# Keeping attention's tile pool open through the up phase, and storing W1's block sums of four groups for the second token half

## The chip, the cores and the metric

The kernel runs on one core of one Trainium2 chip. The metric is the device time of one execution in microseconds (us). A core has five engines that run their own instruction queues: TensorE (PE in the profile, with its weight loads as PEld), VectorE (DVE), ScalarE (ACT), GpSimd (POOL) and SyncE (SP), which here only issues DMA transfers. A transfer issued on SP keeps its place in SP's queue: where it has to wait, everything behind it waits too.

## The reference

One encoder layer over 2048 tokens of width 1024, all in fp32: two mixers in parallel (a Hyena convolution and a bidirectional mLSTM), an output projection, cross-attention into 256 memory tokens, and a feed-forward block of width 4096. Cut to what matters here:

```python
h = h + mixed @ w_out[l]
h = h + _cross_attention(_rms_norm(h, norm_x_g[l]), _rms_norm(mem, norm_mem_g[l]),
                         xa_wq[l], xa_wk[l], xa_wv[l], xa_wo[l])
h = h + jnp.square(jax.nn.relu(_rms_norm(h, norm_ff_g[l]) @ ff_w1[l])) @ ff_w2[l]
...
return _rms_norm(h, final_norm_g)
```

The change lies in the third line, in the product with `ff_w1` (the up phase), and at the end of the second line.

## The kernel before

Every fp32 operand of a product is split into a high part `h` (a cast to fp32r on ACT) and a low part `l` (the rest, a subtraction on DVE or POOL), and one product of blocks is three matmuls: high by high (L340), low by high (L341) and high by low (L342). Names ending in `h` and `l` are these parts: `ah`, `al` of a W1 block, `xh`, `xl` or `bh`, `bl` of a block of tokens.

**Up.** The product with W1 is done in blocks with seven products in place of eight (a Strassen scheme, as `ORDER_UP = (1, 2, 6, 7, 5, 4, 3)`). The tokens come in two halves (`tp` 0 and 1), W1 in 16 groups of columns. For each token half there are seven x operands, one for each product, some of them sums of blocks of x that attention has left in DRAM (`xs`), the others blocks of `hg`, attention's output times the norm's gain. They are split once and then used by all 16 groups. For each group and product there is one W1 operand: four blocks are loaded (L1578), and POOL makes four sums out of them in place (`s` at L1581, `t[1,0]` at L1582, `t[0,0]` at L1590, `t[0,1]` at L1592). One step is one product of one group, four 128x512 blocks deep, and so 12 matmuls; there are 224 steps. The order of the steps is written out as a list: in each token half the first two groups are taken together product by product, the others one by one, and at the end of the first half again two together (14 and 15). In the steps of group 15 of the first half the x operand that has just had its last use is replaced by that of the second half (`ffn_x`). W1 operands are split two steps ahead. The products of a group are added up by DVE (`plus` L1666, `fin` L1671, with two activations L1672 and L1673), POOL makes four sums of the results (L1721 to L1724), and all are stored to DRAM as `hc` (L1662), where the down phase loads them (`wr<-hc`).

**Tile pools.** `T` ("t") belongs to w_out and attention: weights as they come (`wn`, four tiles), their halves `wh` and `wl` (two each), activations `act` (four tiles of 16 KB a partition) and the accumulator `acc` (16 KB). It is closed at the end of attention, and the pool `U` ("up") opens in its place, with the x operands of products 2 to 7, the results `q`, the running sums `u` (six) and the POOL sums `t` (four). `R` ("ring") holds the raw loads `wr` (six slots) and the halves `ah`, `al` (four) and `bh`, `bl` (six). `C` ("wring") holds 12 tiles `w` for W1 blocks. A tile that is asked for waits until the last reader of its slot is done.

**From attention to up.** In attention's last column of tokens (`c == 3`), at its fifth block of output columns (`ct == 4`), `ffn_pre` loads and splits the operands of product 1: x into `bh`, `bl`, and the W1 blocks of products 1 and 2 of groups 0 and 1. It also loads x for product 2 without splitting it. The other x operands are split in the first 12 steps of up, when `U` is there. After the last output block, attention's store of the row statistics `mb` (made by DVE at L1517, stored by SP at L1518) ends that phase; `hg` is stored by ACT's queue (L1488) and the residual by SP (L1490).

The order on each engine is set by a scheduler at build time, from the order of the program, dependencies and its own estimate of each instruction; the pools' slots decide what can be asked for early. `mm3` is the three matmuls, `halves` (L1539, L1540) the split of one block, `raw` (L1534) a load into the ring.

Of the kernel before, what the change touches and what calls it, by code (L numbers as in the profile page):

```python
# [10 lines left out]
F32 = mybir.dt.float32  # L11
F32R = mybir.dt.float32r
# [121 lines left out]
class Prog:  # L134
# [1173 lines left out]
    def attention(self, es):  # L1308
        nc, tc, a = self.nc, self.tc, self.a
# [7 lines left out]
        T = self.T  # L1317
# [51 lines left out]
        mix = mixed(0)  # L1369
        y = next(mix)  # L1370
        stats = None
        acc = T.tile([128, 8, 512], F32, name="acc")
        for c in range(4):

            def residual(h):
# [116 lines left out]
            for ct in range(8):  # L1492
                yield 5.2
                if ct % 2 == 0:
                    w = next(wst) if ct else w
                else:
                    k = sums.pop(0) if sums else None
                    if k is not None:
                        self.sums_x(A, k, "sm")
                if c == 3 and ct == 4:  # L1500
                    self.ffn_pre()
                p = gemm(w, ct, o, half[ct], range(4, 8)) if ct < 2 else gemm(w, ct % 2, o)
                if prev is not None:
                    finish(ct - 1, prev, ssum)
                    store(ct - 1)
                prev = p
# [36 lines left out]
    def ffn_open(self, es):  # L1543
        es.enter_context(self.tc.tile_pool(name="even", bufs=1, side="right")).tile([128, 120], F32, name="even")
        self.R = es.enter_context(self.tc.tile_pool(name="ring", bufs=1, side="right"))
        self.xt = {}
        self.W, self.WD = {}, {}

    def ffn_xload(self, tp, i):
# [3 lines left out]
        return [self.raw(xs[tp, where, :, k] if isinstance(where, int) else hg[2 * tp + where[1], :, 4 * where[0] + k])  # L1553
                for k in range(4)]

    def ffn_x(self, pool, i, src):
        nc = self.nc
        eng = (nc.vector, nc.gpsimd)
        if i == 1:
            self.xt[i] = [self.halves(x, ("bh", "bl"), 6, eng[k % 2]) for k, x in enumerate(src)]  # L1560
            return
        hi, lo = (pool.tile([128, 4, 512], F32R, name=f"x{n}{i}", tag=f"x{n}{i}") for n in "hl")
        for k, raw in enumerate(src):
            nc.scalar.copy(hi[:, k], raw)
            eng[k % 2].tensor_tensor(lo[:, k], raw, hi[:, k].bitcast(F32), ALU.subtract)
        self.xt[i] = [(hi[:, k], lo[:, k]) for k in range(4)]

    def wtile(self):
        return self.C.tile([128, 512], F32, tag="w", name="w", bufs=12)

    def load_w1(self, g):
        op = self.nc.gpsimd.tensor_tensor
        b = self.blocks_of(1, g)
        t = self.W[g] = {}
        for m in (0, 1):
            for k in (1, 0):
                x = self.wtile()
                self.nc.sync.dma_start(out=x.rearrange("p (k c) -> p k c", k=4), in_=b[m][k])  # L1578
                t[m, k] = x
        t["s"] = self.wtile()  # L1580
        op(t["s"], t[1, 0], t[1, 1], ALU.add)  # L1581
        op(t[1, 0], t[0, 0], t[1, 0], ALU.subtract)  # L1582

    def ffn_w1(self, tp, g, i):
        op = self.nc.gpsimd.tensor_tensor
        if i == 1:
            self.load_w1(g)
        t = self.W[g]
        if i == 6:
            op(t[0, 0], t["s"], t[0, 0], ALU.subtract)  # L1590
        if i == 3:
            op(t[0, 1], t[0, 1], t[0, 0], ALU.subtract)  # L1592
        src = t[{1: (0, 0), 2: (0, 1), 6: (0, 0), 7: (1, 0), 5: "s", 4: (1, 1), 3: (0, 1)}[i]]
        return [x.rearrange("p (k c) -> p k c", k=4) for x in self.halves(src, ("ah", "al"), 4, self.nc.vector)]

    def ffn_pre(self):
        self.ffn_x(self.R, 1, self.ffn_xload(0, 1))
        self.wq = []
        for k in range(2):
            for g in range(2):  # L1600
                t = self.R.tile([128, 512], F32, tag="wr", name="wr", bufs=6)
                v = t.rearrange("p (k c) -> p k c", k=4)
                self.nc.sync.dma_start(out=v, in_=self.blocks_of(1, g)[0][k])
                w = self.halves(t, ("ah", "al"), 4, self.nc.vector)
                self.wq.append([x.rearrange("p (k c) -> p k c", k=4) for x in w])
        self.xraw = self.ffn_xload(0, 2)

    def ffn_product(self, aa, i):
        x = self.xt[i]
# [5 lines left out]
    def ffn(self):  # L1615
# [2 lines left out]
        groups = [(0, (0, 1))] + [(0, (g,)) for g in range(2, 14)] + [(0, (14, 15)), (1, (0, 1))]  # L1618
        groups += [(1, (g,)) for g in range(2, 16)]
        steps = [(tp, g, i) for tp, gs in groups for i in self.ORDER_UP for g in gs]  # L1620
        self.C = self.ctx.enter_context(tc.tile_pool(name="wring", bufs=1))
        prods = [(o, i) for o in range(4) for i in self.ORDER_DOWN]
        down = [(n, tp, k) for n in range(len(prods)) for tp in range(2) for k in range(4)]
        aq, bq = {}, {}
# [30 lines left out]
            bq[s] = self.halves(self.raw(hc[tp, i - 1, 4 * o + k]), ("bh", "bl"), 6, eng)  # L1655

        with tc.tile_pool(name="up", bufs=1) as U:
            def tmp():
                return U.tile([128, 512], F32, tag="u", name="u", bufs=6)

            def out(tp, g, j, t):
                nc.sync.dma_start(out=hc[tp, j - 1, g], in_=t)  # L1662

            def plus(p, other):
                t = tmp()
                nc.vector.tensor_tensor(t, p, other, ALU.add)  # L1666
                return t

            def fin(p, other, tp, g, j):
                c = U.tile([128, 512], F32, tag="q", name="q", bufs=7)  # L1670
                nc.vector.tensor_tensor(c, p, other, ALU.add)  # L1671
                nc.scalar.activation(c, c, AF.Relu)  # L1672
                nc.scalar.activation(c, c, AF.Square)  # L1673
                if j:
                    out(tp, g, j, c)
                return c

            wq = self.wq
            xsum = list(range(4, 8))
            us, cs = {}, {}  # L1680
            for n, (tp, g, i) in enumerate(steps):
                if n < 2:
                    self.load_w1(n)
                if n < 12 and n % 2 == 0:
                    j = self.ORDER_UP[n // 2 + 1]
                    self.ffn_x(U, j, self.ffn_xload(0, j) if n else self.xraw)
                if 4 <= n + 2 < len(steps):
                    wq.append(self.ffn_w1(*steps[n + 2]))
                if n + 9 >= len(steps) and n + 5 < len(steps):
                    load_w(0, n + 9 - len(steps))  # L1690
                if n + 2 >= len(steps):
                    k = n + 2 - len(steps)
                    fetch_b(k)
                    fetch_a(0, k)
                if i == 4 and xsum and g % 2 and 2 < g < 13:
                    self.sums_x(U, xsum.pop(0), "t")
                bank = self.ffn_product(wq.pop(0), i) if n > 1 else self.first[n]
                u, c = us.setdefault(g, {}), cs.setdefault(g, {})
                if i == 1:
                    u[1] = tmp()  # L1700
                    nc.scalar.copy(u[1], bank)
                elif i == 2:
                    c[11] = fin(bank, u[1], tp, g, 1)
                elif i == 6:
                    u[2] = plus(bank, u[1])
                elif i == 7:
                    u[3] = plus(bank, u[2])
                elif i == 5:
                    c[22] = fin(bank, u[3], tp, g, 3)
                    u[4] = plus(bank, u[2])  # L1710
                elif i == 4:
                    c[21] = fin(bank, u[3], tp, g, 2)
                else:
                    c[12] = fin(bank, u[4], tp, g, 0)
                    if n + 1 == len(steps):
                        fetch_a(0, 2)
                        fetch_b(2)
                        fetch_a(0, 3)
                    t = [U.tile([128, 512], F32, tag="t", name="t", bufs=4) for _ in range(4)]
                    op = nc.gpsimd.tensor_tensor  # L1720
                    op(t[0], c[12], c[11], ALU.subtract)  # L1721
                    op(t[1], c[22], t[0], ALU.subtract)
                    op(t[2], c[22], c[12], ALU.subtract)
                    op(t[3], c[21], t[1], ALU.subtract)  # L1724
                    for j, x in zip((5, 6, 7, 4), t):
                        out(tp, g, j, x)
                if g == 15 and tp == 0:
                    self.ffn_x(U, i, self.ffn_xload(1, i))
        h2 = self.dram("h2", (4, 128, 8, 512))
        msd = self.dram("msd", (4, 128, 512))  # L1730
        with tc.tile_pool(name="down", bufs=1) as B:
# [155 lines left out]
def program(p):  # L1887
    with ExitStack() as ms:
        with ExitStack() as es:
# [18 lines left out]
            for _ in take(m, 1):  # L1908
                pass
        with ExitStack() as rs:  # L1910
            with ExitStack() as at:
                p.tail_open(at)
                g = p.attention(at)
                weave(g, m, 440, 96, True)
                ms.close()
                p.ffn_open(rs)
                for _ in g:
                    pass
            p.ffn()
# [48 lines left out]
```

## Time and profile before

| | us |
|---|---|
| median of 3 runs | 3202.12 |
| lowest and highest run | 3199.16 and 3203.77 |
| the profiled execution's own time | 3198.5 |
| span of the profiled execution | 3196.7 |
| TensorE busy | 3040.7 |
| DVE busy | 2067.3 |
| ACT busy | 1502.0 |
| POOL busy | 1184.8 |

The span runs from the first to the last instruction that the profiler records; the execution's own time is 1.8 us longer. The mean granted clock of TensorE was 0.982 of full speed. In a line of the profile, `xl<-wr,xh` says what is written from what by the program's names, `x4` counts instructions that the view joins, and the brackets at the end say how long the engine stood idle before and what released it.

### The profile page before, as it was taken

What the parts mean: (1) busy time and instruction counts of PE and PEld (TensorE: products, weight loads), DVE (VectorE), ACT (ScalarE), POOL (GpSimd) and SP (SyncE); (2) the same over time, 40 slices, a digit from 0 to 9 for tenths busy, and PEclk for the clock granted to TensorE, in tenths of its full rate; (3) what the DMA queues carried; (4) which work ended last, traced back from release to release, by engine and by line L of the source; (5) the groups of instructions that cost most, each with busy time, mean ns of one, the idle gap of its engine ahead of it and who ended that gap; (6) DMA issues with size and microseconds to landing.
All of it is one profiled execution on the core that took longest, in us unless ns stands there. A gap on an engine that the chain in (4) does not pass through costs nothing.

```text
span 3196.7 us, 43569 instructions
## 1 busy us (share of the span) xinstructions
PE 3040.7 (95%) x14473; PEld 2391.2 (75%) x14473; DVE 2067.3 (65%) x3563; ACT 1502.0 (47%) x2873; POOL 1184.8 (37%) x818
## 2 busy tenths in 40 slices
PE   6999999999999976999999998999999999999998
PEld 5655566776667766888878887888788878888876
DVE  7775366344874767877775547666655676555695
ACT  5543366424774344454444445555555443333335
POOL 0122012100121334324151218777766483434483
PEclk9999999999999988999999999999999999999999
DMA  5554766686677987556384437655544474444434
GB/s 186 196 198 168 252 195 209 171 266 197 170 231 209 300 269 236 171 169 207 108 295 150 162 120 243 210 195 188 193 153 157 147 248 156 139 135 149 125 93 168
DMA packets 445177, 602.14 MB, mean 188 GB/s; under 512 B 38670, under 2 KB 250766, under 8 KB 443928
## 3 DMA queue, kind: packets, MB, share of 16 engines
q1 hardware_dynamic: 406772, 540.84, 53.2%
q10 hardware_dynamic: 38180, 58.51, 5.5%
q8 instruction: 115, 1.88, 0.2%
q14 instruction: 110, 0.90, 0.1%
HBM read 401.00 MB, written 198.21 MB: 187 GB/s over the span
## 4 chain that ended last, share of the span: by engine, by line
PE 77%; DMA 9%; DVE 7%; issue 3%; ACT 2%; POOL 1%; SPq 1%; ACTq 0%; DVEq 0%; POOLq 0%
PE mm L340 16%; PE mm L341 16%; PE mm L342 16%; PE hy L342 5%; PE hy L340 5%; PE hy L341 5%; PE hy L177 3%; PE hy L876 2%; PE mm L845 1%; PE hy L918 1%; DVE bl L1540 1%; DVE wl L345 1%; PE hy L1082 1%; PE hy L1213 1%; DMA wn<-in_xa_wq_t_dram 1%
## 5 line engine op out<-in xcount | busy, mean ns | idle before, releaser
L345 DVE TENSOR_TENSOR wl<-wn,wh 128x512 fp32r<-128x512 f32 (+1 forms) x364 | 285.7, 820 | 115.8 <-ACT wh L345 115.8
L1540 DVE TENSOR_TENSOR bl<-wr,bh 128x512 fp32r<-128x512 f32 x213 | 236.3, 1115 | 130.8 <-ACT bh L1539 127.1
L345 ACT CAST wh<-wn 128x512 fp32r<-128x512 f32 (+1 forms) x364 | 208.2, 619 | 232.2 <-PE mm L342 56.2
L1539 ACT CAST ah<-w 128x512 fp32r<-128x512 f32 x284 | 176.2, 622 | 300.0 <-PE hy L341 152.1
L923 POOL TENSOR_TENSOR b<-b,a 128x512 f32<-128x512 f32 x64 | 87.8, 1372 | 582.0 <-ACT b L921 459.1
L340 PE MATMUL mm<-xh,wh 128*128 128x512 f32 x640 | 270.6, 424 | 4.5 <-ACT xh L500 2.3
L1540 DVE TENSOR_TENSOR al<-w,ah 128x512 fp32r<-128x512 f32 x236 | 228.6, 970 | 57.4 <-ACT ah L1539 56.9
L341 PE MATMUL mm<-xl,wh 128*128 128x512 f32 x640 | 257.1, 402 | 2.7 <-DVE xl L345 2.2
L342 PE MATMUL mm<-xh,wl 128*128 128x512 f32 x640 | 258.3, 404 | 0.0
L1539 ACT CAST bh<-wr 128x512 fp32r<-128x512 f32 x232 | 143.7, 621 | 235.7 <-PE mm L342 181.4
L342 PE MATMUL mm<-bh,al 128*128 128x512 f32 x576 | 224.0, 391 | 7.0 <-DVE al L1540 4.5
L340 PE MATMUL mm<-bh,ah 128*128 128x512 f32 x576 | 226.0, 392 | 1.7 <-DVE u L1666 1.6
L341 PE MATMUL mm<-bl,ah 128*128 128x512 f32 x576 | 225.1, 391 | 0.0
L341 PE MATMUL mm<-act,wh 128*128 128x512 f32 x512 | 200.5, 392 | 0.2 <-DVE act L345 0.2
L342 PE MATMUL mm<-act,wl 128*128 128x512 f32 x512 | 199.3, 391 | 0.0
L340 PE MATMUL mm<-act,wh 128*128 128x512 f32 x512 | 198.0, 393 | 0.7 <-ACT act L345 0.6
L1389 POOL TENSOR_TENSOR ssum<-ssum,sq 128x512 f32<-128x512 f32 x56 | 81.9, 1462 | 302.9 <-ACT sq L1388 302.9
L340 PE MATMUL hy<-bh,ah 128*128 128x512 f32 x448 | 175.2, 391 | 0.0
L341 PE MATMUL hy<-bl,ah 128*128 128x512 f32 x448 | 174.6, 390 | 0.0
L342 PE MATMUL hy<-bh,al 128*128 128x512 f32 x448 | 174.4, 390 | 0.0
L340 PEld LDWEIGHTS mm<-xh,wh 128*128 128x128 f32 x640 | 121.4, 190 | 65.4 <-issue 29.9
L323 POOL TENSOR_TENSOR b<-b 128x512 f32<-128x512 f32 x32 | 59.1, 1848 | 274.9 <-DVE P L685 126.4
(369 smaller groups left out, 8569.4 us busy)
## 6 DMA issues: line engine op xcount, KB each, us to landing
wr<-hc SPq DMA_DIRECT2D x224, 256.0 KB
w<-in_ff_w_dram SPq DMA_DIRECT2D x176, 256.0 KB
hc<-t SPq DMA_DIRECT2D x128, 256.0 KB
wn<-in_w_in_dram SPq DMA_DIRECT2D x100, 256.0 KB
hc<-q SPq DMA_DIRECT2D x96, 256.0 KB
fs<-a SPq DMA_DIRECT2D x32, 512.0 KB
a<-fs SPq DMA_DIRECT2D x64, 256.0 KB
a<-zs SPq DMA_DIRECT2D x64, 256.0 KB
```

Of the source, the lines that this page charges most:

```text
L177: b = self.nc.tensor.matmul(*products[-1], start=True, stop=True)
L323: nc.gpsimd.tensor_tensor(e[1], f, b, ALU.subtract)
L340: mm(ps, lh, rh, start=start, stop=False)
L341: mm(ps, lh, rl, start=False, stop=False)
L342: mm(ps, ll, rh, start=False, stop=stop)
L345: both = (self.nc.scalar.copy(hi, src), self.nc.vector.tensor_tensor(lo, src, hi.bitcast(F32), ALU.subtract))
L845: nc.tensor.matmul(pp, dm[:, m], t[:, m], start=True, stop=True)
L876: nc.tensor.matmul(pg, em[:, m], y, start=True, stop=True)
L923: nc.gpsimd.tensor_tensor(xt, xt, hi[:, m], ALU.mult)
L1389: nc.gpsimd.tensor_tensor(ssum, ssum, sq, ALU.add)
L1539: self.nc.scalar.copy(hi, src)
L1540: eng.tensor_tensor(lo, src, hi.bitcast(F32), ALU.subtract)
```

## The change

Attention's pool `T` is kept open until the end of up. The x operands of up are written into its tiles: those of products 2, 6, 5 and 4 into `act`, those of 7 and 3 into `wh` and `wl`. So the operands of products 2 and 6 are loaded and split inside attention's last column, after output blocks 3 and 5 begin; that of product 1 and the W1 blocks come there at block 1 instead of 4. The rest are split in steps 0 to 6 of up. The running sums use the eight slices of `acc` in turn in place of six `u` tiles, and the sums of results use `wn` in place of `t`. `wring` lies on the other side of SBUF, so that `T` can close before it.

For groups 0 to 3 the first token half stores the four W1 sums to a DRAM array `w1s` (16 stores of 256 KB on SP's queue). The second half loads one ready block for each product of these groups (28 loads, where there were 16), five steps ahead, and POOL makes no sums for them (16 operations fewer). The matmuls are the same. Lines after the change are shifted: the W1 loads are L1586, the stores of sums L1577, the loads of stored sums L1599, the four sums L1589, L1590, L1611 and L1615.

```diff
-        acc = T.tile([128, 8, 512], F32, name="acc")
+        acc = self.acc = T.tile([128, 8, 512], F32, name="acc")
...
-                if c == 3 and ct == 4:
-                    self.ffn_pre()
+                if c == 3 and ct in (1, 3, 5):
+                    self.ffn_pre(ct // 2)
...
-        hi, lo = (pool.tile([128, 4, 512], F32R, name=f"x{n}{i}", tag=f"x{n}{i}") for n in "hl")
+        if i in (7, 3):
+            hi, lo = (T.tile([128, 8, 256], F32R, tag=t, name="x" + t[1], bufs=2).rearrange("p (k n) c -> p k (n c)", n=2)
+                      for t in ("wh", "wl"))
+        else:
+            x = T.tile([128, 8, 512], F32R, tag="act", name="x", bufs=4)
+            hi, lo = x[:, 0:4], x[:, 4:8]
...
+    def save_w1(self, g, j, t):
+        self.nc.sync.dma_start(out=self.dram("w1s", (4, 4, 128, 512))[g, j], in_=t)
...
         op(t["s"], t[1, 0], t[1, 1], ALU.add)
         op(t[1, 0], t[0, 0], t[1, 0], ALU.subtract)
+        if g < 4:
+            self.save_w1(g, 0, t["s"])
+            self.save_w1(g, 1, t[1, 0])
+
+    def ffn_w1_saved(self, g, i):
+        w, ws = self.blocks_of(1, g), self.dram("w1s", (4, 4, 128, 512))
+        t = self.wtile()
+        src = {1: w[0][0], 2: w[0][1], 4: w[1][1], 5: ws[g, 0], 7: ws[g, 1], 6: ws[g, 2], 3: ws[g, 3]}[i]
+        self.nc.sync.dma_start(out=t.rearrange("p (k c) -> p k c", k=4) if len(src.shape) == 3 else t, in_=src)
+        return t
 
     def ffn_w1(self, tp, g, i):
         op = self.nc.gpsimd.tensor_tensor
+        if tp and g < 4:
+            return [x.rearrange("p (k c) -> p k c", k=4) for x in
+                    self.halves(self.saved.pop(0), ("ah", "al"), 4, self.nc.vector)]
...
         if i == 6:
             op(t[0, 0], t["s"], t[0, 0], ALU.subtract)
+            if g < 4:
+                self.save_w1(g, 2, t[0, 0])
         if i == 3:
             op(t[0, 1], t[0, 1], t[0, 0], ALU.subtract)
+            if g < 4:
+                self.save_w1(g, 3, t[0, 1])
...
-        self.xraw = self.ffn_xload(0, 2)
+        else:
+            i = self.ORDER_UP[part]
+            self.ffn_x(i, self.ffn_xload(0, i))
...
-        self.C = self.ctx.enter_context(tc.tile_pool(name="wring", bufs=1))
+        self.C = self.rs.enter_context(tc.tile_pool(name="wring", bufs=1, side="right"))
...
             def tmp():
-                return U.tile([128, 512], F32, tag="u", name="u", bufs=6)
+                turns[0] += 1
+                return self.acc[:, turns[0] % 8]
...
-                if n < 12 and n % 2 == 0:
-                    j = self.ORDER_UP[n // 2 + 1]
-                    self.ffn_x(U, j, self.ffn_xload(0, j) if n else self.xraw)
+                if n < 8 and n % 2 == 0:
+                    j = self.ORDER_UP[n // 2 + 3]
+                    self.ffn_x(j, self.ffn_xload(0, j))
+                if n + 5 < len(steps) and steps[n + 5][0] and steps[n + 5][1] < 4:
+                    self.saved.append(self.ffn_w1_saved(*steps[n + 5][1:]))
...
-                    t = [U.tile([128, 512], F32, tag="t", name="t", bufs=4) for _ in range(4)]
+                    t = [self.stage() for _ in range(4)]
...
+        self.ts.close()
...
+            p.ts = rs.enter_context(ExitStack())
+            p.tail_open(p.ts)
             with ExitStack() as at:
-                p.tail_open(at)
```

More of the change, by code (lines that the diff above doesn't have):

```diff
@@ L1545, in ffn_open @@
         self.R = es.enter_context(self.tc.tile_pool(name="ring", bufs=1, side="right"))
-        self.xt = {}
+        self.xt, self.rs = {}, es
         self.W, self.WD = {}, {}
@@ L1554, in ffn_xload, with ffn_x @@
                 for k in range(4)]
-    def ffn_x(self, pool, i, src):
-        nc = self.nc
+    def ffn_x(self, i, src):
+        nc, T = self.nc, self.T
         eng = (nc.vector, nc.gpsimd)
@@ L1590, in ffn_w1, with ffn_pre @@
             op(t[0, 0], t["s"], t[0, 0], ALU.subtract)
+            if g < 4:
+                self.save_w1(g, 2, t[0, 0])
         if i == 3:
             op(t[0, 1], t[0, 1], t[0, 0], ALU.subtract)
+            if g < 4:
+                self.save_w1(g, 3, t[0, 1])
         src = t[{1: (0, 0), 2: (0, 1), 6: (0, 0), 7: (1, 0), 5: "s", 4: (1, 1), 3: (0, 1)}[i]]
         return [x.rearrange("p (k c) -> p k c", k=4) for x in self.halves(src, ("ah", "al"), 4, self.nc.vector)]
[L1596 to L1605, printed above, removed]
-        self.xraw = self.ffn_xload(0, 2)
+    def ffn_pre(self, part):
+        if part == 0:
+            self.ffn_x(1, self.ffn_xload(0, 1))
+            self.wq = []
+            for k in range(2):
+                for g in range(2):
+                    t = self.R.tile([128, 512], F32, tag="wr", name="wr", bufs=6)
+                    v = t.rearrange("p (k c) -> p k c", k=4)
+                    self.nc.sync.dma_start(out=v, in_=self.blocks_of(1, g)[0][k])
+                    w = self.halves(t, ("ah", "al"), 4, self.nc.vector)
+                    self.wq.append([x.rearrange("p (k c) -> p k c", k=4) for x in w])
+        else:
+            i = self.ORDER_UP[part]
+            self.ffn_x(i, self.ffn_xload(0, i))
     def ffn_product(self, aa, i):
@@ L1657, in ffn @@
         with tc.tile_pool(name="up", bufs=1) as U:
+            turns = [0]
             def tmp():
-                return U.tile([128, 512], F32, tag="u", name="u", bufs=6)
+                turns[0] += 1
+                return self.acc[:, turns[0] % 8]
             def out(tp, g, j, t):
@@ L1676, in fin @@
                 return c
-            wq = self.wq
+            wq, self.saved = self.wq, []
             xsum = list(range(4, 8))
@@ L1695, in ffn @@
                 if i == 4 and xsum and g % 2 and 2 < g < 13:
-                    self.sums_x(U, xsum.pop(0), "t")
+                    self.sums_x(self.T, xsum.pop(0), "wn")
                 bank = self.ffn_product(wq.pop(0), i) if n > 1 else self.first[n]
@@ L1727, in ffn @@
                 if g == 15 and tp == 0:
-                    self.ffn_x(U, i, self.ffn_xload(1, i))
+                    self.ffn_x(i, self.ffn_xload(1, i))
+        self.ts.close()
         h2 = self.dram("h2", (4, 128, 8, 512))
```

## The prediction

> **What bounds the kernel now.** I read the page first, then busy time by stretch, then TensorE's waits in the stretches that are not full, and last the timeline and the chain of waits there.
>
> ```profile
> span 3196.7 us, 43569 instructions
> PE 3040.7 (95%) x14473; PEld 2391.2 (75%) x14473; DVE 2067.3 (65%) x3563; ACT 1502.0 (47%) x2873; POOL 1184.8 (37%) x818
> PE 77%; DMA 9%; DVE 7%; issue 3%; ACT 2%; POOL 1%; SPq 1%; ACTq 0%; DVEq 0%; POOLq 0%
> ```
>
> TensorE is busy for 95% of the span and carries 77% of the chain. The change takes no matmul away, so only time in which TensorE waits, or runs at a lowered clock, can be won. The next view is busy time in stretches of 50 us (columns: PE, weight loads, DVE, ACT, POOL, granted clock, DMA share, GB/s).
>
> ```profile
> 1850.00:1900.00 50.00, 50.00 (x237) 41.76 (x236) 26.37 (x50) 24.86 (x52) 6.44 (x5) 1.00 0.33 114
> 1900.00:1950.00 50.00, 39.69 (x154) 30.00 (x153) 27.37 (x27) 21.00 (x38) 31.05 (x21) 0.86 0.66 210
> 1950.00:2000.00 50.00, 50.00 (x222) 41.44 (x221) 39.29 (x45) 29.52 (x51) 40.71 (x29) 1.00 0.75 246
> 2200.00:2250.00 50.00, 44.84 (x190) 36.07 (x189) 44.36 (x45) 33.34 (x60) 41.73 (x26) 0.95 0.72 226
> 2600.00:2650.00 50.00, 45.54 (x195) 37.25 (x194) 39.32 (x35) 18.10 (x33) 44.69 (x30) 0.97 0.65 215
> ```
>
> Where attention ends (row 1850) and just after the start of up (row 1950) TensorE is full. It is idle for 10.3 us in 1900 to 1950 (attention to up), 5.2 us in 2200 to 2250 (the second token half begins) and 4.5 us in 2600 to 2650 (up to down). The change touches the first two. What ends TensorE's idle time there (the first four rows are 1905 to 1960, the last two 2200 to 2260; total, times, longest):
>
> ```profile
> PE hy L340 <- ACT ah L1539: 6.1, 2, 4.2
> PE hy L341 <- POOL xl L1565: 2.6, 1, 2.6
> PE hy L342 <- DVE al L1540: 0.9, 2, 0.6
> PE hy L340 <- ACT xh L1564: 0.8, 1, 0.8
> ...
> PE hy L342 <- DVE al L1540: 3.3, 2, 2.2
> PE hy L340 <- ACT ah L1539: 1.9, 1, 1.9
> ```
>
> At the first place 3.4 us (2.6 and 0.8) are waits for x operands and 7.0 us (6.1 and 0.9) for W1 operands. At the second all 5.2 us are for W1 operands. The timeline and the chain (the last four rows) say what stands behind them at the first place.
>
> ```profile
> 1912.36 2.03 SPq L1578 DMA_DIRECT2D w<-in_ff_w_dram  x4
> 1913.92 0.69 DVE L1517 TENSOR_SCALAR mb<-hy 128x512 f32<-128x512 f32 x1 [5.62 <-PE hy L1512]
> 1916.49 3.41 SPq L1578 DMA_DIRECT2D w<-in_ff_w_dram  x4
> 1920.08 1.26 POOL L1581 TENSOR_TENSOR w<-w 128x512 f32<-128x512 f32 x1 [2.77 <-DMA w<-in_ff_w_dram]
> 1925.52 1.26 POOL L1590 TENSOR_TENSOR w<-w 128x512 f32<-128x512 f32 x1
> 1927.82 0.61 ACT L1539 CAST ah<-w 128x512 fp32r<-128x512 f32 x1
> 1928.49 0.79 PE L340 MATMUL hy<-xh,ah 128*128 128x512 f32 x1 [4.16 <-ACT ah L1539]
> 1934.70 1.27 POOL L1590 TENSOR_TENSOR w<-w 128x512 f32<-128x512 f32 x1
> 1936.68 0.50 PE L340 MATMUL hy<-xh,ah 128*128 128x512 f32 x1 [1.89 <-ACT ah L1539]
> ...
> 1913.88 6.07 DMA w<-in_ff_w_dram
> 1923.75 4.17 DMA w<-in_ff_w_dram
> 1939.92 0.43 PE hy L342
> 1942.45 0.23 PE mm L341
> ```
>
> The four W1 blocks of group 0 are issued from 1912.36, POOL starts its sums at 1920.08 (7.7 us later), the third sum, the operand of product 6, is done at 1926.78, its cast starts at 1927.82 and TensorE at 1928.49. Group 1 repeats this: third sum done at 1935.97, TensorE at 1936.68. After the long wait a matmul takes 0.43 instead of 0.23 us in the chain. Products 6 of the two groups are 24 such matmuls, so the lowered clock costs about 24 x 0.20 = 4.8 us more. All that can be won at this place is about 10.3 + 4.8 = 15 us.
>
> The Trainium skill (TensorE: Matmul & The Clock Gate, "What's actually happening") says that TensorE falls to half speed after about 3.4 us idle and needs as long busy to come back. Row and rule agree here (half speed after a wait of 4.16 us), and the rule speaks against this change as far as it joins short waits into one long one: by it the wait of about 8 us found below would be followed by half speed once more, and none of the 4.8 us would come back.
>
> **The change, part by part.** *Attention's last column.* The operands of products 2 and 6 are now loaded and split inside it: 8 casts of 0.61 us on ACT, 4 subtractions on DVE and 4 on POOL. In 1850 to 1900 ACT has 25 us free, DVE 24 and POOL 44, so the work fits. The casts stand in ACT's queue between softmax and the casts that feed TensorE's last attention products. In the changed order TensorE has 18 matmuls (18 x 0.23 = 4.1 us) ahead of the ones that need them, against 8 x 0.61 = 4.9 us of casts if all stood in one piece. I take 0.3 us lost, with bounds 0 and 2 (two loads that land late and hold ACT).
>
> *Attention to up.* The 3.4 us of waits for x go. What is late next is the W1 chain, which the change does not shorten. In the new order of SP's queue the four loads of group 0 stand behind the store of `mb` (L1518), which waits for DVE L1517 to end at 1914.61. They also wait for the last store of `hg`. So they are issued about 1915.1 instead of 1912.36, 2.8 us later, and POOL can start at about 1922.8 if the landing takes the same 7.7 us. Its three sums then run without the x subtractions that lay between them before: 1922.8 + 3 x 1.26 = 1926.6, against 1926.78. The cast on ACT stands behind five casts of x operands, one of which waits for its load. TensorE starts product 6 between 1927 and 1928.5 (before: 1928.49), after one wait of about 8 us, because product 2 now ends near 1920. In group 1, two of the four loads stand on SP behind the new store of the first sum, which waits for POOL. POOL has seven operations between group 0's third sum and the end of group 1's third (three subtractions of x, the last sum of group 0, and three sums) at 1.26 to 1.74 us: 1926.6 + 8.8 to 12.2, with the third sum at 1936 to 1939 (before: 1935.97). TensorE starts there between 1936.7 and 1939.7 (before 1936.68). I take +1.5 us, the middle, with the slow matmuls as before. The bounds are -4 (the four loads land in 4.17 us, the chain's other load of W1, since eight x loads no longer go with them) and +7 (2.8 us for the later issue and one landing of 4.17 us more behind the store).
>
> The 16 stores that the first half adds (4 for each of groups 0 to 3) cost an issue on SP each and 4 MB of DMA time. In 1950 to 2000 TensorE is full at a DMA share of 0.75, so I cost them at nothing. If that cover is gone, one landing of 4.17 us shows on TensorE for the load that it holds back.
>
> *The token-half switch.* Here are the two stretches around the waits, and POOL's and DVE's groups in 2219 to 2253.
>
> ```profile
> 2219.00:2233.00 14.00, 14.00 (x63) 11.57 (x63) 12.93 (x14) 10.56 (x19) 11.59 (x8) 1.00 0.73 221
> 2233.00:2252.00 19.00, 13.84 (x50) 10.29 (x49) 18.04 (x16) 13.37 (x25) 19.00 (x13) 0.82 0.65 205
> ...
> L1592 POOL TENSOR_TENSOR w<-w 128x512 f32<-128x512 f32 x2 | 3.5, 1736 | 0.0
> L1590 POOL TENSOR_TENSOR w<-w 128x512 f32<-128x512 f32 x2 | 3.4, 1743 | 0.0
> L1582 POOL TENSOR_TENSOR w<-w 128x512 f32<-128x512 f32 x1 | 1.7, 1735 | 0.0
> L1581 POOL TENSOR_TENSOR w<-w 128x512 f32<-128x512 f32 x1 | 1.3, 1293 | 6.9 <-DMA w<-in_ff_w_dram 6.9
> ...
> L1565 DVE TENSOR_TENSOR xl<-wr,xh 128x512 fp32r<-128x512 f32 x7 | 11.1, 1623 | 3.0 <-ACT xh L1564 3.0
> ...
> 1915.40 0.69 DVE L1565 TENSOR_TENSOR xl<-wr,xh 128x512 fp32r<-128x512 f32 x1 [0.34 <-ACT xh L1564]
> 2242.99 0.62 ACT L1539 CAST bh<-wr 128x512 fp32r<-128x512 f32 x1 [2.41 <-DMA wr<-hc]
> 2247.16 0.79 PE L342 MATMUL hy<-xh,al 128*128 128x512 f32 x1 [2.25 <-DVE al L1540]
> ```
>
> In 2233 to 2252 POOL is busy for all 19.00 us and DVE for 18.04: here the two are the bound, and TensorE waits for `al` (2247.16). The same subtraction takes DVE 0.69 us with POOL idle (1915.40) and 1.62 us on average here: each overlap with POOL costs it about 0.9 us. The Trainium skill (SBUF — State Buffer, "SBUF: two separate sides") says that DVE operations with two SBUF inputs and GpSimd operations take turns on one pair of ports; the rows agree. Six of the eight sums of groups 0 and 1 lie in this stretch, 9.9 us of POOL, and all go. So DVE is freed of about 6 x 0.9 = 5.4 us, more than the 5.2 us of waits for `al` and `ah`, of which 1.9 come from a cast held behind a load (2242.99) that is issued earlier when POOL frees its ring slot earlier. The matmuls after 2247.16 ran slow too, 12 x 0.20 = 2.4 us. All that is to be had is 5.2 + 2.4 = 7.6 us. I take 6.5, since an end of one operand remains that is last. Against it stand 14 loads instead of 8 for the pair, 1.5 MB more in about 38 us, 40 GB/s on top of 221. The sum, 261, lies below the 275 that the next fence shows. Bounds: 0 (the loads take back all) and 7.6.
>
> ```profile
> 1920.00:1942.00 22.00, 12.44 (x33) 8.06 (x32) 15.72 (x13) 12.82 (x23) 21.92 (x15) 0.69 0.87 275
> 2215.55 9.22 SPq L1534 DMA_DIRECT2D wr<-xs  x4
> ```
>
> The second row is the risk: SP stood 9.2 us over four x loads waiting for ring slots, and the new W1 loads are in the same queue. They are issued 5 steps (5 x 12 x 0.23 = 13.8 us) ahead, and in the changed order each stands ahead of x loads of its own product, so x stays the later one.
>
> *Up to down* keeps its order on SP and its loads: 0, with bounds of 2 either way (the tile pool closes before down).
>
> **Sum.** 0.3 + 1.5 - 6.5 + 0 = -4.7 us. The profiled execution took 3198.5 us for its span of 3196.7; the change makes it 3193.8. The median of the runs, 3202.1, lies 3.6 above it, so I forecast 3202.1 - 4.7 = 3197.4. About 0.2% (6.4 us) is what a measurement can tell from no change, the runs themselves lying 4.6 us apart.
>
> **Rivals.** *Both places close.* Without eight x loads beside them the W1 blocks land in 4.17 us: the first place gains 4 and keeps its clock, 4.8 more, and with 6.5 at the switch the sum is -15, 3187. For it: the DMA share is 0.87 in 1920 to 1942. Against it: the later issue, and x loads that still follow at once.
>
> *The gain is hidden.* Loads from the first half's sums come late behind SP's ring waits and the switch keeps its waits for `ah`: 0.3 + 1.5 - 1 = +0.8, 3203. For it: the 9.22 us row. Against it: the order above.
>
> *Slower: SP's queue holds W1 back.* The stores of sums wait for POOL in an in-order queue and the loads of the next group stand behind them. Group 0 starts 2.8 us later, group 1 another 4.17 after it, and 24 more matmuls run at half speed, 4.8: +11.8. With the switch at -3 it is +9, 3211. It decides when group 1's product 6 starts after 1936.7 + 6.5 = 1943.2, from which point it eats the whole gain of the switch. For it: POOL is busy 21.92 of 22 us there. Against it: only two of group 1's loads stand behind a store.
>
> **Numbers.** The forecast has 0.52, both places closing 0.22, the hidden gain 0.13, slower 0.13. The forecast alone spans 3192 to 3202 (its bounds in part against each other). The range of 3187 to 3206 leaves out the lower end of the first rival and most of the last, less than 0.2. Faster by over 0.2% (below 3195.7) are the first rival and 0.2 of the forecast, 0.42; slower by as much is the last rival and a tail, 0.14; the rest, 0.44, is within.
>
> **What would show it.** Right: no wait of TensorE for `xl` or `xh` between 1910 and 1925; one wait of about 8 us for `ah` ending near 1928; six fewer POOL operations around 2219 to 2253, DVE's subtractions nearer to 1.2 us, TensorE's busy time in 2200 to 2250 near 49; no change in 1950 to 2200. Wrong: the first product 6 starts before 1925 or after 1931; TensorE waits in 1950 to 2200; waits for `w` loads from the stored sums at the switch; a new gap in 1850 to 1910.

## The result, and the profile after

The median was 3195.36 us over 10 runs, against 3200.80 us over 10 runs of the kernel before: ratio 0.9978 (95% interval 0.9969 to 0.9987), or -7.0 us (-9.9 to -4.2); the medians lie 5.4 us apart. The forecast was -4.7 us and 3197.4. The profiled execution has a span of 3193.7 us, 3.0 less than the one before.

The page of the changed kernel:

```profile
span 3193.7 us, 43601 instructions
PE 3050.3 (96%) x14473; PEld 2399.5 (75%) x14473; DVE 2056.9 (64%) x3563; ACT 1503.6 (47%) x2873; POOL 1156.5 (36%) x802
```

TensorE has the same 14473 matmuls, POOL 16 operations fewer. Busy time by stretches of 50 us (PE, weight loads, DVE, ACT, POOL, granted clock, DMA share, GB/s):

```profile
1850.00:1900.00 50.00, 50.00 (x237) 41.46 (x236) 32.25 (x54) 28.50 (x60) 10.94 (x9) 1.00 0.37 121
1900.00:1950.00 50.00, 38.50 (x144) 29.40 (x143) 22.59 (x23) 19.26 (x34) 28.16 (x21) 0.80 0.79 260
1950.00:2000.00 50.00, 50.00 (x223) 41.39 (x222) 31.18 (x42) 27.24 (x45) 34.37 (x24) 1.00 0.76 253
2200.00:2250.00 50.00, 48.88 (x216) 40.14 (x215) 45.82 (x48) 35.77 (x65) 36.45 (x23) 1.00 0.85 279
```

Attention's last column stays full although ACT, DVE and POOL do more there (row 1850). The place where attention ends is no better: 38.50 us busy against 39.69, clock 0.80 against 0.86. The switch of token halves is where the gain lies: 48.88 against 44.84. TensorE's waits in 1880 to 1960 (first two rows) and in 2200 to 2270:

```profile
PE hy L340 <- ACT ah L1539: 8.7, 2, 7.6
PE hy L342 <- DVE al L1540: 2.8, 2, 1.9
...
PE hy L342 <- DVE al L1540: 1.1, 1, 1.1
```

No wait for `xl` or `xh` is left where attention ends. In its place stands one wait of 7.6 us for a W1 operand. At the switch 1.1 us is left of 5.2.

To compare kernels place by place I use one more number, worked out from all matmul starts of a trace: by how much the distance from one start to the next is longer than at full rate (0.2266 us for 128x512, in proportion for narrower ones), summed over a stretch. It holds waits and slow matmuls, and does not depend on how long the phases ahead took. Between executions of the same code these shift the start of attention's last column by several us: the 8800th matmul starts 1.8 us later in this profile than before, and the spans of two profiles of the changed kernel were 3193.7 and 3195.5, of the kernel before 3196.7 and 3199.8. In us:

| profile | last column (1840 to 1912) | attention to up (1905 to 1960) | switch (2190 to 2300) | up to down (2500 to 2700) |
|---|---|---|---|---|
| before, first and second | 1.8, 1.8 | 17.4, 17.7 | 8.3, 8.2 | 8.8, 8.3 |
| changed, first and second | 2.1, 2.1 | 19.5, 17.2 | 1.5, 1.2 | 8.4, 11.0 |
| pool part alone (e1) | 2.1 | 21.0 | 8.7 | 7.3 |
| stored sums alone (e2) | 1.8 | 17.4 | 1.5 | 9.0 |
| POOL kept busy (e3) | 2.1 | 17.8 | 8.0 | 6.3 |
| group 0's blocks early (e4) | 2.1 | 13.7 | 1.4 | 9.0 |
| both groups' blocks early (e5) | 2.1 | 3.3 | 1.7 | 9.5 |
| two groups stored (e6) | 2.1 | 18.1 | 2.3 | 7.6 |
| POOL busy with memsets (e7) | 2.6 | 19.6 | 5.3 | 8.1 |

Between 1960 and 2190 every one of these profiles lost less than 0.1 us. Up to down varies by up to 4.7 us with no pattern that follows a kernel. In e7 the last column's 2.6 holds 0.5 us from behind that column, which this execution reached 3.5 us sooner than the first profile of the changed kernel, and so before 1912; without them it is 2.1 as in the others.

### The profile page after: what moved, and what is told of

It is laid out like the page before. It is cut to its first block, busy times and chain, and to the rows that moved or that the text cites. A ratio compares the mean times of both kernels' runs of the same rounds, so it can differ in the third digit from the quotient of the medians.

```text
span 3193.7 us, 43601 instructions
## 1 busy us (share of the span) xinstructions
PE 3050.3 (96%) x14473; PEld 2399.5 (75%) x14473; DVE 2056.9 (64%) x3563; ACT 1503.6 (47%) x2873; POOL 1156.5 (36%) x802
## 3 DMA queue, kind: packets, MB, share of 16 engines
q8 instruction: 115, 1.88, 0.3%
## 4 chain that ended last, share of the span: by engine, by line
PE 76%; DMA 9%; DVE 7%; issue 3%; ACT 3%; POOL 1%; SPq 1%; ACTq 0%; DVEq 0%; POOLq 0%
PE mm L340 16%; PE mm L342 16%; PE mm L341 16%; PE hy L342 5%; PE hy L340 5%; PE hy L341 5%; PE hy L177 3%; PE hy L876 1%; PE mm L845 1%; PE hy L918 1%; DVE wl L345 1%; DMA xt<-in_x_t_dram 1%; PE hy L1213 1%; PE hy L1215 1%; DMA wn<-in_xa_wq_t_dram 1%
## 5 line engine op out<-in xcount | busy, mean ns | idle before, releaser
L1540 DVE TENSOR_TENSOR al<-w,ah 128x512 fp32r<-128x512 f32 x236 | 218.7, 928 | 53.6 <-ACT ah L1539 53.5
L1389 POOL TENSOR_TENSOR ssum<-ssum,sq 128x512 f32<-128x512 f32 x56 | 82.2, 1467 | 254.5 <-ACT sq L1388 252.6
L341 PEld LDWEIGHTS mm<-xl,wh 128*128 128x128 f32 x640 | 121.4, 190 | 51.6 <-issue 24.2
```

Of the source, the lines that this page charges most:

```text
L341: mm(ps, lh, rl, start=False, stop=False)
L1389: nc.gpsimd.tensor_tensor(ssum, ssum, sq, ALU.add)
L1540: eng.tensor_tensor(lo, src, hi.bitcast(F32), ALU.subtract)
```

## The experiments

**The two parts alone.** e1 is the changed kernel without the stored sums:

```diff
-        if g < 4:                                   # four places
+        if g < 0:
...
-                if n + 5 < len(steps) and steps[n + 5][0] and steps[n + 5][1] < 4:
+                if n + 5 < len(steps) and steps[n + 5][0] and steps[n + 5][1] < 0:
```

> The changed kernel without its second part: the pool is kept open, W1's sums are made by POOL in both token halves, nothing is stored or loaded for them. Theory (the gain of 6.9 us at the token-half switch comes from the sums that POOL no longer makes, and the pool part costs about 2.4 us where attention ends): the waits at the switch are back, about 8 us lost there, the place where attention ends stays as in the changed kernel, time 1 to 4 us above the kernel before (ratio 1.000 to 1.001). Rival (the operands' new buffers help at the switch, since they come free at other times): the switch keeps 4 us or more of its gain and the time is 2 us or more below the kernel before.

e2 is the kernel before with `save_w1`, `ffn_w1_saved` and their calls put in as in the diff of the change, its pools unchanged.

> The kernel before with the second part of the change alone: its pools are as they were, the W1 sums of groups 0 to 3 are stored and loaded again. Theory: the switch loses about 1.5 us in place of 8.3, and the place where attention ends stays as before but for the stores of sums in SP's queue (0 to +2 us there): 5 to 7 us below the kernel before, ratio 0.998. Rival (both parts are needed, the earlier operands free the loads that the switch needs): the switch gains less than 3 us.

e1 came to ratio 1.0017 (1.0007 to 1.0026), +5.4 us; e2 to 0.9984 (0.9973 to 0.9994), -5.1 us. TensorE's waits at the switch, of e1 and then of e2:

```profile
PE hy L342 <- DVE al L1540: 4.8, 1, 4.8
PE hy L340 <- ACT ah L1539: 0.8, 2, 0.5
```

```profile
PE hy L342 <- DVE al L1540: 1.2, 1, 1.2
```

The switch loses 8.7 us with the pool part alone and 1.5 with the stored sums alone, as the theory had it. The rivals of both fall: the new buffers give nothing there, and the stored sums don't need them. The pool part is a loss by itself: its 21.0 us where attention ends are 3.4 more than the 17.6 of before. Its time, +5.4 us (2.2 to 8.3), lies somewhat above the 1 to 4 us expected; this is one profile, and that place differs by 2.3 us between two profiles of the changed kernel. The new stores of sums are not needed for that cost: e1 has none, and TensorE's two waits for `ah` there were 7.0 and 3.9 us, against 7.6 and 1.1 in the changed kernel. The times of the two parts do not add up either: +5.4 and -5.1 make about nothing, where the two together measured -7.0. By place, part of this is e1's 21.0 us, more than any profile with both parts lost there; why it is so high stays open.

**Is it POOL's work, or the chain of load, sum and cast?** e3 gives POOL eight additions back that nothing waits for (not shown: the tile `idle` that they write is made, and set to zero once, at the start of up):

```diff
+        if tp and g < 2:
+            for _ in range(int(i in (6, 7, 5, 4))):
+                op(self.idle, self.idle, self.saved[0], ALU.add)
         if tp and g < 4:
             return [x.rearrange("p (k c) -> p k c", k=4) for x in
```

> The changed kernel with eight additions put back on POOL at the switch (one for each of products 6, 7, 5 and 4 of groups 0 and 1 in the second half). They read the loaded block and write a tile that nothing reads, so no cast waits for them. Theory (POOL's own work is what held TensorE, by slowing DVE's subtractions of two SBUF operands and by delaying POOL's own subtractions of x): DVE's subtractions between the two token halves are back at 1.5 to 1.75 us, and 4 to 7 us of the 6.9 come back there. Rival (what counted was the chain from load to sum to cast, which is gone here too): the switch stays within 2 us of the changed kernel.

Ratio 1.0006 (0.9996 to 1.0016): the gain is gone. Busy time around the switch, of the changed kernel and then of e3, each with DVE's two groups of x subtractions in 2219 to 2253:

```profile
2219.00:2233.00 14.00, 14.00 (x64) 11.58 (x63) 12.51 (x16) 11.25 (x21) 7.45 (x5) 1.00 0.89 259
2233.00:2252.00 19.00, 17.88 (x79) 14.50 (x78) 17.91 (x16) 13.75 (x27) 17.09 (x12) 1.00 0.84 289
...
L1570 DVE TENSOR_TENSOR x<-wr,x 128x512 fp32r<-128x512 f32 x4 | 5.6, 1420 | 0.3 <-ACT x L1569 0.3
L1570 DVE TENSOR_TENSOR xl<-wr,xh 128x512 fp32r<-128x512 f32 x4 | 4.9, 1224 | 0.5 <-ACT xh L1569 0.5
```

```profile
2219.00:2233.00 14.00, 14.00 (x63) 11.61 (x62) 14.00 (x15) 9.43 (x18) 12.95 (x8) 1.00 0.72 220
2233.00:2252.00 19.00, 14.14 (x50) 10.57 (x50) 17.98 (x16) 13.63 (x26) 18.84 (x13) 0.82 0.88 289
...
L1570 DVE TENSOR_TENSOR x<-wr,x 128x512 fp32r<-128x512 f32 x4 | 7.0, 1779 | 0.0
L1570 DVE TENSOR_TENSOR xl<-wr,xh 128x512 fp32r<-128x512 f32 x4 | 6.4, 1628 | 0.0
```

With POOL full again (12.95 of 14 us and 18.84 of 19) DVE's subtractions are back from 1.32 us on average to 1.70, DVE has no idle time in the first stretch, and TensorE loses 8.0 us as before. All of 6.6 us comes back; the chain, which is as short here as in the changed kernel, gives nothing by itself. The load of stored blocks is no hindrance either: in the changed kernel no cast of a W1 operand between 2215 and 2254 waits for one.

**Which side of POOL's work?** It can slow DVE beside it, or hold up POOL's own subtractions of x and with them the ring slots. e7 keeps POOL as long at work without reading:

```diff
-                op(self.idle, self.idle, self.saved[0], ALU.add)
+                op(self.idle[:, 0:1], self.idle[:, 0:1], self.saved[0][:, 0:1], ALU.add)
+                self.nc.gpsimd.memset(self.idle, 0.0)          # 128x1728
```

> As in the experiment that kept POOL busy at the switch, but each of the eight additions is now a one-column addition (which places it) and a memset of 1728 columns, of about 1.55 us, so that POOL is as long at work but reads next to nothing from SBUF meanwhile. Theory (DVE's two-operand subtractions are slowed by POOL's reading): DVE's subtractions stay near the changed kernel's 1.3 us and the switch loses no more than 3 us, in place of 8.0 with the additions. Rival (POOL's own subtractions of x come late behind its other work, whatever that is): 6 us or more are lost there, with DVE's subtractions short.

The switch lost 5.3 us, between the two; ratio 0.9994 (0.9984 to 1.0004). Its DVE groups of x subtractions and the added POOL groups in 2219 to 2253, and rows of the timeline that tell the sides apart:

```profile
L1570 DVE TENSOR_TENSOR xl<-wr,xh 128x512 fp32r<-128x512 f32 x3 | 4.2, 1420 | 2.6 <-ACT xh L1569 2.6
L1570 DVE TENSOR_TENSOR x<-wr,x 128x512 fp32r<-128x512 f32 x4 | 3.8, 959 | 0.1
...
L1607 POOL MEMSET idle<- 128x1728 f32 x6 | 9.3, 1548 | 0.2
L1606 POOL TENSOR_TENSOR idle<-idle,w 128x1 f32<-128x1 f32 x5 | 2.1, 412 | 0.2
...
2221.25 0.68 DVE L1540 TENSOR_TENSOR al<-w,ah 128x512 fp32r<-128x512 f32 x1
2230.62 1.43 DVE L1570 TENSOR_TENSOR x<-wr,x 128x512 fp32r<-128x512 f32 x2
2243.33 1.75 DVE L1540 TENSOR_TENSOR al<-w,ah 128x512 fp32r<-128x512 f32 x1
...
2220.24 1.55 POOL L1607 MEMSET idle<- 128x1728 f32 x1
2230.07 1.56 POOL L1607 MEMSET idle<- 128x1728 f32 x1
2242.82 1.71 POOL L1762 TENSOR_TENSOR wn<-q 128x512 f32<-128x512 f32 x1
...
2233.68 0.62 ACT L1569 CAST x<-wr 128x512 fp32r<-128x512 f32 x1 [2.36 <-DMA wr<-xs]
...
2245.13 0.50 PE L342 MATMUL hy<-x,al 128*128 128x512 f32 x1 [2.46 <-DVE al L1540]
2246.28 0.63 PE L340 MATMUL hy<-x,ah 128*128 128x512 f32 x1
```

DVE's subtractions of x are short (1.16 us on average). The subtraction at 2221.25 ran at its 0.68 us though most of it lay beside a memset, and so did the two from 2230.62, 1.43 us together. The Trainium skill (SBUF — State Buffer, "SBUF: two separate sides") has a DVE operation with two SBUF inputs wait only for GpSimd operations that read SBUF; these rows agree. Yet TensorE waits: POOL's x subtractions come late, loads of x get their ring slots late, and ACT stands 2.36 us at a cast whose load has not landed, with the W1 casts behind it. TensorE's longest wait, 2.46 us, then ends with a W1 subtraction (2243.33) that took 1.75 us beside one of POOL's sums of results (2242.82). W1 subtractions took 1.12 us on average, as in the changed kernel. So both sides count: of the 6.6 us, 3.9 come back when the added work reads next to nothing, and 2.7 more when it reads. That is no clean split. The one-column additions took POOL another 2.1 us here, which e3 did not have, so 3.9 may be too much, and what comes late on POOL still slows DVE further on.

**Where attention ends.** e4 loads group 0's four W1 blocks early:

```diff
+        if part == 2:
+            b = self.blocks_of(1, 0)
+            self.early = [self.load_block(self.stage(), b[m][k]) for m in (0, 1) for k in (1, 0)]
...
-                x = self.wtile()
-                self.nc.sync.dma_start(out=x.rearrange("p (k c) -> p k c", k=4), in_=b[m][k])
-                t[m, k] = x
+                t[m, k] = self.early.pop(0) if self.early and not g else self.load_block(self.wtile(), b[m][k])
```

> The changed kernel with the four W1 blocks of group 0 loaded during attention's last column into the weight tiles of the pool that is kept, instead of after attention into the ring. Theory (where attention ends, W1's chain of load, three sums and a cast is the last wait, and not the operands of x): the long wait of 7.8 us shrinks to below 2 us, the wait for group 1's operand remains (2 to 5 us), matmuls run at full speed for longer; 8 to 14 us less than the changed kernel's 19.5 us lost there, ratio to the kernel before 0.9935 to 0.996. Rival (casts and subtractions of x on ACT, DVE and POOL hold the operands whatever the loads do): less than 4 us gained.

Ratio 0.9973 (0.9962 to 0.9983). The place lost 13.7 us, 5.8 less than in the first profile of the changed kernel: short of the 8 to 14 expected, and only 3.5 less than in the second profile, so that e4 alone does not rule out the rival (less than 4). Waits in 1905 to 1960 and the two rows of TensorE at which product 6 begins:

```profile
PE hy L340 <- ACT ah L1539: 6.6, 2, 4.9
PE hy L342 <- DVE al L1540: 0.9, 2, 0.7
...
1928.13 0.50 PE L340 MATMUL hy<-x,ah 128*128 128x512 f32 x1 [1.76 <-ACT ah L1539]
1937.72 0.80 PE L340 MATMUL hy<-x,ah 128*128 128x512 f32 x1 [4.86 <-ACT ah L1539]
```

Group 0's wait fell from 7.60 to 1.76 us, and group 1's grew from 1.09 to 4.86. TensorE had only come sooner to the next block that was late. e5 goes on from there: group 1's blocks are loaded and both groups' sums begun in attention too, with nine of the ring's 12 tiles opened ahead of attention's last column.

```diff
+            self.load_w1(0)
+            self.load_w1(1)
...
+        self.C1 = es.enter_context(self.tc.tile_pool(name="wring1", bufs=1, side="right"))
...
-                if n < 2:
-                    self.load_w1(n)
```

> The changed kernel with the W1 blocks of groups 0 and 1 loaded, and POOL's sums of them begun, inside attention's last column: group 0's blocks in the weight tiles of the kept pool as in the last experiment, group 1's in nine tiles of the W1 ring that are opened before attention ends (the other three after it). Theory (W1's chain of load, three sums and a cast is the last wait for both groups): the waits for the operands of product 6 go in both groups, no wait over 3 us is left, the clock stays up, and 3 to 7 us in all are lost there, in place of 19.5 in the changed kernel and 13.7 with group 0's blocks early; ratio to the kernel before 0.993 to 0.996. Rival (the operands of x, with the casts on ACT, are the next wait right behind): 10 us or more are lost there still.

Ratio 0.9949 (0.9934 to 0.9963), -16 us: the fastest version here. The place lost 3.3 us, 14 to 16 less than in the two profiles of the changed kernel. By the ratios (0.9949 against 0.9978) the difference is some 9 us; both are loose, to about 5 and 3 us, and no row accounts for the rest. All that TensorE waited for in 1895 to 1960, and the stretch:

```profile
PE hy L1512 <- POOL ssum L1389: 1.7, 1, 1.7
```

```profile
1900.00:1950.00 50.00, 48.33 (x215) 39.51 (x215) 27.66 (x35) 26.78 (x48) 35.94 (x25) 1.00 0.94 314
```

No operand is waited for, and the clock is 1.00 throughout. The 1.7 us are attention's own: its last sum on POOL (L1389) now stands behind sums of W1. W1's chain was the last wait in both groups; the x operands, on time since the change, are not the next one.

**How many groups count.** e6 stores groups 0 and 1 alone (`g < 2` for `g < 4`).

> The changed kernel with the sums of groups 0 and 1 alone stored and loaded (8 stores and 14 loads in place of 16 and 28). Theory (only the sums beside the x subtractions of the second half count): the switch loses 1 to 2 us as in the changed kernel, and the time is the changed kernel's within 2 us, ratio to the kernel before 0.997 to 0.9985. Rival (the sums of groups 2 and 3 count as well, POOL being still full when they start): 3 us or more come back at the switch.

The switch lost 2.3 us, against 1.5 and 1.2: about 6 of the 6.9 us gained there are from the two groups. The time does not say so: ratio 0.9992 (0.9984 to 1.0000), where 0.997 to 0.9985 was expected. No place in up accounts for the difference to the changed kernel's 0.9978, and the intervals touch; it stays open.

**How far profiles of one kernel differ.** Both kernels were profiled once more.

> The kernel before once more, for a second profile: how far the time lost at each place differs between executions of one kernel. Expected within 1.5 us at each of the three places of up (17.4, 8.3 and 8.8 us in the first profile).

> The changed kernel once more, for a second profile. Expected within 1.5 us of the first at each place (19.5 us where attention ends, 1.5 at the switch, 8.4 before down). If the change costs nothing where attention ends, it comes nearer to the 17.4 of the kernel before there.

The kernel before repeats within 0.5 us at each place. The changed kernel does not, and misses the 1.5 us expected: 19.5 and 17.2 where attention ends, 8.4 and 11.0 before down. The switch repeats within 0.3 us in both.

## Why the prediction was right

**Attention's last column.** +0.3 was taken and +0.3 measured, in every kernel with the pool part.

**Attention to up.** +1.5 was taken. The two profiles give +2.1 and -0.5; with e3, e6 and e7, whose code for these two groups is the same but for a memset in e3 and e7, the mean is 18.4 against 17.6, +0.9. The sequence was as told, though 1.7 us later, as this execution reached the place later:

```profile
1916.30 0.32 SPq L1518 DMA_DIRECT2D msd<-mb  x1
1916.86 2.11 SPq L1586 DMA_DIRECT2D w<-in_ff_w_dram  x4
1922.78 1.26 POOL L1589 TENSOR_TENSOR w<-w 128x512 f32<-128x512 f32 x1 [3.75 <-DMA w<-in_ff_w_dram]
1925.46 1.26 POOL L1611 TENSOR_TENSOR w<-w 128x512 f32<-128x512 f32 x1
1925.74 0.62 ACT L1569 CAST xh<-wr 128x512 fp32r<-128x512 f32 x1 [2.42 <-DMA wr<-xs]
1928.87 0.61 ACT L1539 CAST ah<-w 128x512 fp32r<-128x512 f32 x1
1929.53 0.80 PE L340 MATMUL hy<-x,ah 128*128 128x512 f32 x1 [7.60 <-ACT ah L1539]
1936.44 1.28 POOL L1611 TENSOR_TENSOR w<-w 128x512 f32<-128x512 f32 x1
1938.42 0.80 PE L340 MATMUL hy<-x,ah 128*128 128x512 f32 x1 [1.09 <-ACT ah L1539]
```

The loads stand behind the store of `mb`. They landed sooner than taken (5.9 us from issue to the first sum, not 7.7), and group 0's third sum was done at 1926.72. The cast then stood behind casts of x, one of which waited 2.42 us for its load. Product 6 started at 1929.53 and 1938.42; less the 1.7 us of the later start that is 1927.8 and 1936.7, inside the predicted 1927 to 1928.5 and at the lower end of 1936.7 to 1939.7. For group 0 this is in part luck: the blocks landed 1.8 us sooner than taken, and the cast came 2.15 us after the third sum (1926.72 to 1928.87), where the prediction had left 0.4 to 1.9 us from that sum to TensorE; the two errors all but cancel. Two of the prediction's figures are a little off without changing the sum: 1926.6 + 8.8 is 1935.4, not 1936, and by the spacing of starts the two places had 17.4 and 8.3 us to win, not 15 and 7.6.

The Trainium skill's rule (TensorE: Matmul & The Clock Gate, "What's actually happening"), half speed after about 3.4 us idle, fits this place: after 7.60 us idle a clock of 0.80 in that stretch, and with no wait over 1.7 us in e5 a clock of 1.00. At the switch the measurement differs: in e7 a single wait of 2.46 us was enough, and matmuls started 0.43 in place of 0.23 us apart from 2246.28 on. In the kernel before 2.25 us were enough (at 2247.16), with a wait of 1.88 shortly ahead. After the 1.1 us left in the changed kernel the clock stayed at 1.00. So waits shorter than 3.4 us must be counted too.

**The switch.** -6.5 was taken; -6.8 and -7.0 were measured, and 48.88 us busy against "near 49". DVE's subtractions took 1.32 us in place of 1.62, not quite the 1.2 told. The size was right, its make-up only in part: the prediction put 5.4 us on DVE being slowed, where e7 puts about 2.7 on POOL's reading and the larger share, as far as its rough split goes, on POOL's own work coming late and the ring slots with it, for which the prediction had named one cast and 1.9 us. The added loads raised the stretch to 278 GB/s, more than the 261 predicted, at no cost.

**The rivals.** Both places closing needed W1's blocks earlier, as e5 shows; fewer x loads beside them were not enough. The hidden gain and the slower case did not come: group 1's product 6 started at 1938.42, before 1943.2.

**The sum.** By place the first pair of profiles gives 0.3 + 2.1 - 6.8 - 0.4 = -4.8 us against -4.7 forecast. That they agree to 0.1 us is chance: the terms of attention to up and up to down differ by 2.3 and 2.6 us between two profiles of the changed kernel. The measured ratio says -7.0 (-9.9 to -4.2), which holds -4.7.

## What to carry to other kernels

Follow a wait to the operand that is last, not to the one that is named most: x operands waited 3.4 us in the profile, and taking these away gained nothing, since W1's chain ended later; moving that chain took 14 to 16 us off what that place lost. Where two engines are full beside each other, as here at the switch, work taken off the one can pay twice, in the other's speed and in the ring slots that it frees. Where phases ahead shift by more than the effect, compare two profiles place by place, by the spacing of matmul starts, and not by their spans.

## What was not expected of the hardware

A memset on POOL left DVE subtractions of two SBUF operands at their 0.68 us in e7, where e3's additions on POOL brought those of x to 1.70 on average; the prediction had made no difference between POOL's operations. TensorE fell to half speed after a single wait of 2.46 us in e7. And DMA moved 314 GB/s over 50 us in e5, with TensorE at full clock and hardly waiting, above the 275 that the prediction took as its mark. That mark was no limit: the page of the kernel before has 300 GB/s in one of its slices of 80 us, with TensorE busy for nine tenths of it.
